# A decoder trunk in split fp32: two more pairs of blocks as seven products, another order of the recurrent steps, and pairs and softplus at other blocks

## Chip, cores and metric

One Trainium2 core runs the kernel in one launch. The metric is device time in microseconds. The kernel before took 1047.36 us as the median of three runs (1046.35 to 1047.64).

## The reference

Two layers work on x of 256 tokens by 1024 features, in float32. Every layer has a feed-forward (SwiGLU), a mixer and a second feed-forward, each followed by a residual sum and a LayerNorm:

```python
x = layer_norm(ALPHA * x + 0.5 * swiglu(x, w_in, w_out), g, b)   # d_ff 2816
x = layer_norm(ALPHA * x + mixer(x), g, b)
x = layer_norm(ALPHA * x + 0.5 * swiglu(x, w_in, w_out), g, b)

def swiglu(x, w_in, w_out):
    gate, up = jnp.split(x @ w_in, 2, axis=-1)
    return (jax.nn.silu(gate) * up) @ w_out
```

The mixer of the first layer is a gated linear recurrence over 1280 channels in five groups of 256: `log_a = -8 * sigmoid(gates0) * softplus(-lam)`, `a = exp(log_a)`, `b = sqrt(-expm1(2 * log_a)) * sigmoid(gates1) * u`, `h = scan(a, b)`, and `(gelu(y) * h) @ w_out`, where u is a short causal convolution. The mixer of the second layer is attention over three dilated windows, on keys and values projected once from the output of the first layer.

## The kernel before

**Products.** Nothing fits in SBUF for long: all weights stream from HBM in halves of 128x1024 float32. Each half is split in two parts of type float32r: the scalar engine (ACT) casts it to the high part (L130), the vector engine (DVE) subtracts that from the original to get the low part (L131). A product is three matmuls, high by high, high by low and low by high (`mm3`, L93). Six buffers hold raw halves and nine the split ones (`RAWBUFS`, `WBUFS`), so ACT and DVE may run up to nine halves ahead of TensorE.

**A feed-forward** (`ffn`, L402) walks over eleven blocks of 256 of its 2816 columns. A normal block j takes four halves of `w_in`, 48 matmuls of 512 columns, then a silu on ACT, the gate on DVE, four transposes, and a split of the result; with it go two halves of `w_out` for block j-2, 24 matmuls into the sums `yy`. The last three pieces of `w_out` come at the end, with the LayerNorm behind them (`Project.finish`).

**Pairs** (`combined` L330, `two_blocks` L438) do two neighbouring blocks together with seven products in place of eight, in Strassen's manner with fewer sums (Winograd's form): a product is 12 matmuls. The halves of the weights that the products need are sums and differences of raw halves, made by DVE in place (L342, eight per pair) and then split as others are (L107, L108: fourteen halves per pair, where two normal blocks have eight). The matching sums of x, `s1` to `s4`, are made once per feed-forward (`sum_x`, L407: eight sums on DVE, four splits). `PAIRS` says which blocks begin a pair: in the first feed-forward 4 and 8, in the second and fourth 3 and 7, in the third none.

**The recurrent part** (L616) runs a list of steps, `RG` (L602), and keeps ACT, DVE and GpSimd in the program's order (`pinned`, L159). `uN` and `yN` are projections (48 matmuls of 256 columns), `cN` the convolution, `gN` the gate products (16 matmuls), `hN` the sigmoids, `bN` the exp and tanh, `aN` a sum on DVE, `qN` the square root, `mN` a product, `sN` the scan, `eN` a copy of y, `zN` its gelu, `FN` the product of both, `kN` its split, `oN` the output projection, which reads what `kN` wrote. `pv` prepares one more half of weights ahead; `pV` does so too, but with the cast on DVE and not on ACT. `T` and its digits say how many halves are prepared at the points of `finish`.

**What sets the order elsewhere.** Outside the pinned parts a list scheduler places the instructions of each engine, by the order of the program and by what is ready in its own reckoning. Each engine then runs its list strictly in that order, and so does the DMA queue of the sync engine. TensorE's list keeps the program's order throughout.

Of the kernel before, what the change touches and what calls it, by code (L numbers as in the profile page):

```python
# [10 lines left out]
F32R = mybir.dt.float32r  # L11
AF = mybir.ActivationFunctionType
ALU = mybir.AluOpType

P = 128
# [13 lines left out]
NO_SYNC = mybir.DependencyInfo(mybir.DependencyClass.NoSync, mybir.DependencyReason.DATA)  # L29
# [6 lines left out]
TAIL = 3  # L36
WBUFS = 9
RAWBUFS = 6
PAIRS = {0: (4, 8), 1: (3, 7), 3: (3, 7)}
KVBUFS = 12  # L40
WARM = 17
PRE = 2
LATE = 5
HBUFS = 6
DILATIONS = ((128, 1), (512, 4), (2048, 16))
SLOPES = [float(2.0 ** (-8.0 * (i + 1.0) / HEADS)) for i in range(HEADS)]
# [3 lines left out]
def trunk_kernel(  # L50
# [21 lines left out]
    nc = tc.nc  # L72
# [3 lines left out]
    act = ctx.enter_context(tc.tile_pool(name="act", bufs=1))  # L76
# [38 lines left out]
    def at(pair, *idx):  # L115
        return pair[0][(slice(None),) + idx], pair[1][(slice(None),) + idx]

    barrier = {}

    def half_piece(src, low=nc.vector, cuts=1, high=nc.scalar):  # L120
        if low is None:
            w = wts.tile([P, HALF], F32, name="w_full", tag="w_hi", bufs=WBUFS)
            nc.sync.dma_start(w, src)
            return w
        raw = wts.tile([P, HALF], F32, name="raw", bufs=RAWBUFS)
        w = duo("w", WBUFS, wts, (HALF,))
        for n in range(cuts):
            c = slice(n * HALF // cuts, (n + 1) * HALF // cuts)
            nc.sync.dma_start(raw[:, c], src[:, c])
            (nc.scalar.copy if high is nc.scalar else high.tensor_copy)(w[0][:, c], raw[:, c])  # L130
            i = low.tensor_tensor(out=w[1][:, c], in0=raw[:, c], in1=f32(w[0][:, c]), op=ALU.subtract)  # L131
        if low in barrier:
            tc.add_manual_dep(i.ins, barrier[low].ins.name, NO_SYNC, reason="after the LayerNorm")
        return w
# [17 lines left out]
    def take(n=2):  # L152

        pump(n - len(ready))
        w, ready[:n] = ready[:n], []
        return w
# [69 lines left out]
    def load_ln(i, tag="o", bufs=4):  # L226
        gb = [[act.tile([P, 512], F32, name="gb", tag=f"{tag}_{('hi', 'lo')[j]}", bufs=bufs) for j in range(2)]
              for _ in range(2)]
        for r in range(2):
            for h in range(2):  # L230
                tc.keep_in_program_order(
                    nc.sync.dma_start(gb[r][h], ln[i, r, h * 512:(h + 1) * 512].partition_broadcast(P)))
        return gb
# [145 lines left out]
    def order_ffn(idx):  # L379
# [4 lines left out]
        for j in range(NJ):  # L384
            if j - 1 in PAIRS.get(idx, ()):
                continue
            if j in PAIRS.get(idx, ()):
                sums = combined(idx, j)
# [10 lines left out]
        for i in range(NJ - TAIL, NJ):  # L399
            order(w_out[idx, i])  # L400

    def ffn(ln_i, turn_x, ahead, pairs=()):  # L402
        hs, gated = {}, {}
        later = []
        sums = {}

        def sum_x():  # L407

            sums["tmp"] = v = [act.tile([P, 4, P], F32, name="v", tag="kv", bufs=KVBUFS) for _ in range(4)]

            def whole(dst_, q, t):
                hi, lo = at(xT, slice(4 * q, 4 * q + 4), tok(t))
                nc.vector.tensor_tensor(dst_, f32(hi), f32(lo), ALU.add)

            def keep(name, src):
                pair = [act.tile([P, 4, P], F32R, name="s", tag="kv", bufs=KVBUFS) for _ in range(2)]
                split(pair[0], pair[1], src)
                sums[name] = pair

            whole(v[0], 0, 0)  # L420
            whole(v[1], 0, 1)
            nc.vector.tensor_tensor(v[2], v[0], v[1], ALU.subtract)
            keep("s3", v[2])
            whole(v[3], 1, 1)
            nc.vector.tensor_tensor(v[1], v[1], v[3], ALU.add)
            keep("s1", v[1])
            nc.vector.tensor_tensor(v[0], v[1], v[0], ALU.subtract)
            keep("s2", v[0])
            whole(v[3], 1, 0)
            nc.vector.tensor_tensor(v[3], v[3], v[0], ALU.subtract)  # L430
            keep("s4", v[3])
# [6 lines left out]
        def two_blocks(j):  # L438

            xs = [act_.rearrange("p k s -> p (k s)") for act_ in sums["tmp"]]  # L440
            flat = lambda n: xs[n]
            part = lambda q, t: (lambda k: at(xT, 4 * q + k, tok(t)))
            named = lambda n: (lambda k: at(sums[n], k))
            a, b, c = (bank() for _ in range(3))
            product(a, part(0, 0), True, False)
            nc.scalar.copy(flat(0), a)
            product(c, named("s1"), True, False)
            nc.scalar.copy(flat(1), c)
            flush()
            product(b, named("s2"), True, False)  # L450
            nc.vector.tensor_tensor(flat(2), b, flat(0), ALU.add)
            product(c, named("s4"), False)
            nc.vector.tensor_tensor(flat(3), c, flat(2), ALU.add)
            gate(flat(3), 0, j + 1)
            w = take()
            for t in range(NT):
                prj.part(t, j - 2, w)
            product(b, named("s3"), False, False)
            nc.vector.tensor_tensor(flat(2), b, flat(0), ALU.add)
            nc.vector.tensor_tensor(flat(1), flat(1), flat(2), ALU.add)  # L460
            gate(flat(1), 1, j + 1)
            product(a, part(1, 0), False)
            gate(a, 0, j)
            product(b, part(1, 1), False)
            nc.vector.tensor_tensor(flat(0), b, flat(0), ALU.add)
            flush()
            gate(flat(0), 1, j)
            w = take()
            for t in range(NT):
                prj.part(t, j - 1, w)  # L470

# [3 lines left out]

        def gate(ps, t, j):
            sg = work.tile([P, 256], F32, name="sg")
            nc.scalar.activation(sg, ps[:, :256], AF.Silu)  # L478
            if t == 0:
                gated[j] = work.tile([P, NT, 256], F32, name="gated", tag="sc")  # L480
            nc.vector.scalar_tensor_tensor(gated[j][:, t, :], ps[:, 256:], 0.5, sg, ALU.mult, ALU.mult)  # L481

            def rest():
                hh = gated.pop(j)
                pt = bank()
                for m in range(2):
                    for t_ in range(NT):
                        turn(pt[:, (m * NT + t_) * P:(m * NT + t_ + 1) * P], hh[:, t_, m * P:(m + 1) * P])
                split(*hs[j], halves(pt))
            if t:  # L490
                later.append(rest)

        prj = Project(lambda t, k: at(hs[k // 2], k % 2, tok(t)), KF)
        for j in range(2):
            hs[j] = duo("h", HBUFS)
        if turn_x:
            gb = load_ln(ln_i)
            w = [take() for _ in range(3)]
            opened = []
            for t in range(NT):  # L500
                ps = bank()
# [5 lines left out]
                ps = bank()  # L507
# [9 lines left out]
        else:  # L517
            with pinned():
                ps = [[bank() for _ in range(NT)] for _ in range(2)]
                for q in range(4):  # L520
# [4 lines left out]
                    for j in range(2):  # L525
                        w = take(1)
# [8 lines left out]
                    if j == 0:  # L535
                        pump(4 - PRE)
        for j in range(2, NJ):
            if j == LATE and not turn_x:
                late_loads()
                gb = load_ln(ln_i)  # L540
                softplus_prep()
            if j - 1 in pairs:
                continue
            hs[j] = duo("h", HBUFS)
            if j in pairs:
                hs[j + 1] = duo("h", HBUFS)
                two_blocks(j)
                continue
            w = [take() for _ in range(2)]
            for t in range(NT):  # L550
                ps = bank()
                natural(ps, t, w)
                flush(1 - t if j == 2 else 0)
                gate(ps, t, j)
            if j == 2 and pairs:
                sum_x()
            if 0 <= j - 2 < NJ - TAIL:
                w = take()
                for t in range(NT):
                    prj.part(t, j - 2, w)  # L560
        for i in range(NJ - 2, NJ - TAIL):
            w = take()
# [21 lines left out]
    def natural_pair(turn_x, then):  # L584
# [3 lines left out]
        for t, ps in enumerate(natural_both(turn_x)):  # L588
# [3 lines left out]
            def rest(t=t, tmp=tmp):  # L592
# [6 lines left out]

    ENGINES = {"v": (nc.vector, nc.scalar), "g": (nc.gpsimd, nc.scalar),  # L600
               "V": (nc.vector, nc.vector), "G": (nc.gpsimd, nc.vector)}
    RG = """pv u3 pv pv pv r0 pv pv r1 c1 pv u2 pv u4 pv c0 g0 pv c2 pv pv c4 pv g1 pv pv h0 h1 pv y0 pv c3 e0 pv  # L602
        g2 h2 b2 y1 pv b0 g3 pv h3 pv pv g4 h4 y2 pv a2 b4 b1 b3 a01 y3 q01 a34 e2 q34 y4 z0 m01 e1 z1 s0 s1
        m4 F1 F0 z2 pv e4 k0 k1 z4 e3 q2 s4 m3 o0 m2 z3 s2 F4 F2 o1 s3 k2 o2 pv F3 pv k4 k3 T21101""".split()

    def order_recurrent():
        both = (nc.vector, nc.vector)
# [349 lines left out]
    order_ffn(3)  # L957

    turn_x = ffn(0, None, 4, PAIRS.get(0, ()))
    with pinned():  # L960
        turn_x = recurrent(1, turn_x)
    turn_x = ffn(2, turn_x, 4, PAIRS.get(1, ()))
    kv = keys_values(turn_x)
    pump(6)
    turn_x = ffn(3, lambda h: None, 4)
    with pinned():
        turn_x = attention(kv, 4, turn_x)
    ffn(5, turn_x, 0, PAIRS.get(3, ()))

# [75 lines left out]
```

## Time and profile before

| what | value |
|---|---|
| median of the runs (three) | 1047.36 us |
| the profiled execution, its own time | 1048.89 us |
| its span, first to last instruction | 1047.1 us |
| TensorE busy | 1019.5 us, 97% |
| DVE busy | 774.5 us, 74% |
| ACT busy | 568.7 us, 54% |
| mean granted clock of TensorE | 0.995 |
| HBM read | 190.75 MB, 183 GB/s over the span |

The stages can be told from the matmuls: first feed-forward to about 194 us, recurrent part to 308, second feed-forward to 495, keys and values to 545, third feed-forward to 725, attention to 858, fourth feed-forward to the end. TensorE is nearly always busy, so the places that count are the few where it waits, and the number of its matmuls. A share of 74% for DVE is a mean over stages between 50% and 97%.

### The profile page before, as it was taken

Reading aid. Unit: us, or ns where it says so; the run is one execution under the profiler, and the core shown is the slowest. Engines: PE = TensorE matmul, PEld = TensorE weight load, DVE = VectorE, ACT = ScalarE, POOL = GpSimd, SP = SyncE. Lnnn points to the kernel's source line nnn. Section 1 sums busy time; section 2 is a strip of 40 time slices with the busy share of each in tenths; the row PEclk is TensorE's granted clock in tenths of the full one; section 3 lists DMA queues with packets and bytes.
Section 4 is the critical chain, followed back from the end, with each engine's and each line's share of the span. In section 5 each row is a group of like instructions: output and inputs, shape, how many; then the busy total and the mean of one; then the engine's idle time right before and its main releaser. Section 6 shows DMA issues by size and latency. Waiting matters only on the chain.

```text
span 1047.1 us, 13806 instructions
## 1 busy us (share of the span) xinstructions
PE 1019.5 (97%) x5233; PEld 853.4 (82%) x5233; DVE 774.5 (74%) x997; ACT 568.7 (54%) x790; POOL 12.0 (1%) x18
## 2 busy tenths in 40 slices
PE   8999999999899999999999999999999999999997
PEld 6787887899777888888898888888998778888885
DVE  6979877686789888777736454557677889888864
ACT  5647555359955564654435344442776755564740
POOL 0000000000000000000000000000000000000000
PEclk9999999999899999999999999999999999999999
DMA  8639458175263483672756555642533544483641
GB/s 300 243 103 339 158 195 305 62 281 173 84 228 141 138 272 140 230 286 101 263 200 203 198 186 177 200 164 99 182 122 121 181 141 151 141 281 132 240 161 41
DMA packets 55650, 192.70 MB, mean 184 GB/s; under 512 B 6432, under 2 KB 6688, under 8 KB 55584
## 3 DMA queue, kind: packets, MB, share of 16 engines
q1 hardware_dynamic: 55584, 191.83, 53.4%
q8 instruction: 41, 0.67, 0.3%
q14 instruction: 25, 0.20, 0.1%
HBM read 190.75 MB, written 1.05 MB: 183 GB/s over the span
## 4 chain that ended last, share of the span: by engine, by line
PE 83%; DVE 7%; ACT 3%; DMA 3%; issue 2%; POOL 0%; SPq 0%; DVEq 0%; ACTq 0%; POOLq 0%
PE mm L91 51%; PE yy L91 29%; PE mm L101 3%; DVE w_lo L131 2%; DMA raw<-in_w_in_dram 2%; DVE w_lo L108 1%; DMA raw<-in_w_out_dram 1%; ACT w_hi L130 1%; DVE xn L257 1%; DVE xT L108 1%; DVE xn L244 1%; DVE st L245 1%; ACT th L104 1%; ACT w_hi L107 0%; ACT L104 0%
## 5 line engine op out<-in xcount | busy, mean ns | idle before, releaser
L131 DVE TENSOR_TENSOR w_lo<-raw,w_hi 128x1024 fp32r<-128x1024 f32 (+1 forms) x295 | 352.1, 1217 | 118.0 <-ACT w_hi L130 111.2
L91 PE MATMUL mm<-w_hi,xT 128*128 128x512 f32 x1296 | 417.6, 393 | 2.6 <-DVE gated L481 1.2
L130 ACT CAST w_hi<-raw 128x1024 fp32r<-128x1024 f32 (+1 forms) x294 | 301.5, 1048 | 178.1 <-PE yy L91 70.6
L91 PEld LDWEIGHTS mm<-w_hi,xT 128*128 128x128 f32 x1296 | 242.8, 188 | 57.3 <-DVE xT L108 2.9
L91 PE MATMUL mm<-w_lo,xT 128*128 128x512 f32 x648 | 253.0, 390 | 2.2 <-DVE w_lo L131 2.2
L91 PEld LDWEIGHTS mm<-w_lo,xT 128*128 128x128 f32 x648 | 121.8, 188 | 28.0 <-DVE w_lo L131 4.0
L91 PE MATMUL yy<-w_hi,h_hi 128*128 128x512 f32 x352 | 138.9, 395 | 0.0
L91 PE MATMUL yy<-w_lo,h_hi 128*128 128x512 f32 x352 | 137.3, 390 | 0.0
L91 PE MATMUL yy<-w_hi,h_lo 128*128 128x512 f32 x352 | 137.3, 390 | 0.0
L107 ACT CAST w_hi<-raw 128x1024 fp32r<-128x1024 f32 x84 | 86.0, 1052 | 65.4 <-DVE raw L342 31.1
L108 DVE TENSOR_TENSOR w_lo<-raw,w_hi 128x1024 fp32r<-128x1024 f32 x84 | 100.6, 1219 | 14.4 <-ACT w_hi L107 14.0
L91 PE MATMUL mm<-xT,w_hi 128*128 128x256 f32 x480 | 88.6, 286 | 0.0
L91 PEld LDWEIGHTS yy<-w_lo,h_hi 128*128 128x128 f32 x352 | 66.2, 188 | 14.1 <-DVE w_lo L131 0.8
L91 PEld LDWEIGHTS yy<-w_hi,h_lo 128*128 128x128 f32 x352 | 66.1, 188 | 13.9
L91 PEld LDWEIGHTS yy<-w_hi,h_hi 128*128 128x128 f32 x352 | 66.1, 188 | 13.1
L91 PEld LDWEIGHTS mm<-xT,w_hi 128*128 128x128 f32 x480 | 74.7, 191 | 2.4 <-issue 2.0
L478 ACT ACTIVATE sg<-mm 128x256 f32<-128x256 f32 x70 | 26.6, 381 | 88.1 <-PE mm L91 87.8
L91 PE MATMUL mm<-xT,w_lo 128*128 128x256 f32 x240 | 67.9, 283 | 0.0
L481 DVE SCALAR_TENSOR_TENSOR gated<-mm,sg 128x256 f32<-128x256 f32 x70 | 29.1, 419 | 47.0 <-ACT sg L478 47.0
L91 PE MATMUL mm<-w_hi,s 128*128 128x512 f32 x192 | 62.7, 393 | 0.0
L342 DVE TENSOR_TENSOR raw<-raw 128x1024 f32<-128x1024 f32 x48 | 57.7, 1218 | 1.8 <-DMA raw<-in_w_in_dram 1.6
L91 PEld LDWEIGHTS mm<-xT,w_lo 128*128 128x128 f32 x240 | 45.9, 191 | 0.0
(132 smaller groups left out, 995.0 us busy)
## 6 DMA issues: line engine op xcount, KB each, us to landing
raw<-in_w_in_dram SPq DMA_DIRECT2D x175, 512.0 KB, 4.9
raw<-in_w_out_dram SPq DMA_DIRECT2D x88, 512.0 KB, 5.0
raw<-in_q_w_dram SPq DMA_DIRECT2D x20, 512.0 KB, 4.5
raw<-in_rg_in_dram SPq DMA_DIRECT2D x16, 512.0 KB, 4.8
gb<-in_ln_dram SPq DMA_DIRECT2D x24, 256.0 KB, 5.7
raw<-in_rg_out_dram SPq DMA_DIRECT2D x10, 512.0 KB, 3.9
raw<-in_v_w_dram SPq DMA_DIRECT2D x8, 512.0 KB, 5.1
raw<-in_k_w_dram SPq DMA_DIRECT2D x8, 512.0 KB, 5.6
```

Of the source, the lines that this page charges most:

```text
L91: tc.keep_in_program_order(nc.tensor.matmul(ps, lhsT=lhsT, rhs=rhs, start=start, stop=stop, **kw))
L101: tc.keep_in_program_order(nc.tensor.transpose(ps, src, ident))
L104: tc.keep_in_program_order(nc.scalar.activation(dst_, src, f, **kw))
L107: nc.scalar.copy(hi, src)
L108: nc.vector.tensor_tensor(lo, src, f32(hi), ALU.subtract)
L130: (nc.scalar.copy if high is nc.scalar else high.tensor_copy)(w[0][:, c], raw[:, c])
L131: i = low.tensor_tensor(out=w[1][:, c], in0=raw[:, c], in1=f32(w[0][:, c]), op=ALU.subtract)
L244: nc.vector.scalar_tensor_tensor(z, z, ALPHA, y, ALU.mult, ALU.add)
L245: nc.vector.bn_stats(self.st[:, h, :], z)
L342: nc.vector.tensor_tensor(raw[out, h], raw[x, h], raw[y, h], ALU.subtract)
L478: nc.scalar.activation(sg, ps[:, :256], AF.Silu)
L481: nc.vector.scalar_tensor_tensor(gated[j][:, t, :], ps[:, 256:], 0.5, sg, ALU.mult, ALU.mult)
```

## The change

Four edits. (1) `PAIRS` gets an entry for the third feed-forward, (3, 7), so four of its blocks are done as two pairs; the sums `s1` to `s4` have their homes in the buffers named o and h there, since keys and values hold eight of the twelve kv buffers. (2) In the first feed-forward the pairs begin at 5 and 8 rather than at 4 and 8, `sum_x` is called before the first pair rather than at block 2, and `softplus_prep` at block 7 rather than 5. (3) `ahead_of`: the first weight half that ACT casts for the block after a pair must come behind the silu of the pair's second block, half t = 1. (4) `RG` is another order of the same steps, with 11 of its 26 `p` steps as `pV`, and T22001 for T21101.

```diff
-PAIRS = {0: (4, 8), 1: (3, 7), 3: (3, 7)}
+PAIRS = {0: (5, 8), 1: (3, 7), 2: (3, 7), 3: (3, 7)}
+SOFTPLUS = 7
...
-            (nc.scalar.copy if high is nc.scalar else high.tensor_copy)(w[0][:, c], raw[:, c])
+            i = (nc.scalar.copy if high is nc.scalar else high.tensor_copy)(w[0][:, c], raw[:, c])
+            if high in ahead_of:
+                tc.add_manual_dep(i.ins, ahead_of.pop(high).ins.name, NO_SYNC, reason="after the gate")
...
-                pair = [act.tile([P, 4, P], F32R, name="s", tag="kv", bufs=KVBUFS) for _ in range(2)]
+                pair = [act.tile([P, 4, P], F32R, name="s", tag=tag, bufs=bufs) for tag, bufs in homes[len(sums) - 1]]
...
-            gate(flat(1), 1, j + 1)
+            silu = gate(flat(1), 1, j + 1)
...
             w = take()
+            ahead_of[nc.scalar] = silu
             for t in range(NT):
                 prj.part(t, j - 1, w)
...
-            if j == LATE and not turn_x:
+            if not turn_x and j == LATE:
                 late_loads()
                 gb = load_ln(ln_i)
+            if not turn_x and j == SOFTPLUS:
                 softplus_prep()
...
-            if j == 2 and pairs:
+            if pairs and j == pairs[0] - 1:
                 sum_x()
...
-    RG = """pv u3 pv pv pv r0 pv pv r1 c1 pv u2 pv u4 pv c0 g0 pv c2 pv pv c4 pv g1 pv pv h0 h1 pv y0 pv c3 e0 pv
...
+    RG = """u4 pv pV pv pv pV pv pv r0 pV r1 u3 C0 u2 c1 pV g0 C2 pv g1 y0 c3 pv pv g2 pV pv h0 C4 pv y1 g4 pv e0
...
-    turn_x = ffn(3, lambda h: None, 4)
+    o_pair, h_pair = (tuple((f"{tag}_{part}", bufs) for part in ("hi", "lo")) for tag, bufs in (("o", 4), ("h", HBUFS)))
+    turn_x = ffn(3, lambda h: None, 4, PAIRS.get(2, ()), 2 * (o_pair,) + 2 * (h_pair,))
```

What this does to the engines' lists is shown at three places. Line numbers of the changed kernel are 1 to 7 higher.

First, ACT at the end of the second pair of the first feed-forward; before:

```order
L107 CAST w_hi<-raw 128x1024 x2
L130 CAST w_hi<-raw 128x1024 x5
L478 ACTIVATE sg<-v 128x256
L478 ACTIVATE sg<-mm 128x256
L130 CAST w_hi<-raw 128x1024 x2
L107 CAST h_hi<-mm 128x512
L478 ACTIVATE sg<-v 128x256
L130 CAST w_hi<-raw 128x1024 x4
```

and of the change:

```order
L108 CAST w_hi<-raw 128x1024 x3
L131 CAST w_hi<-raw 128x1024 x2
L482 ACTIVATE sg<-v 128x256
L482 ACTIVATE sg<-mm 128x256
L131 CAST w_hi<-raw 128x1024 x2
L108 CAST h_hi<-mm 128x512
L131 CAST w_hi<-raw 128x1024
L482 ACTIVATE sg<-v 128x256
L131 CAST w_hi<-raw 128x1024 x6
```

The silu (`sg<-v`) had five casts of weights ahead of it that were not the pair's own products, and has two.

Second, ACT in the recurrent part, from the table load of the square roots (`th<-th`) to the first split of a result that `o0` reads (`kv<-y`); before:

```order
L104 ACT_TABLE_LOAD
L104 ACTIVATE th<-th 128x512 x2
L655 COPY y<-yy 128x512
L104 ACTIVATE th<-th 128x512 x2
L104 ACT_TABLE_LOAD
L104 ACTIVATE y<-y 128x512
L655 COPY y<-yy 128x512
L104 ACTIVATE y<-y 128x512 x2
L130 CAST w_hi<-raw 128x1024
L655 COPY y<-mm 128x512
L107 CAST kv<-y 128x512 x2
```

and of the change:

```order
L105 ACT_TABLE_LOAD
L105 ACTIVATE th<-th 128x512 x4
L105 ACT_TABLE_LOAD
L105 ACTIVATE y<-y 128x512
L661 COPY y<-yy 128x512 x2
L105 ACTIVATE y<-y 128x512 x2
L108 CAST kv<-y 128x512
```

A cast of weights and a copy that stood before the split are gone from there. Earlier on the list, a block's exp and tanh (four instructions) and the casts between the last sigmoids and the table load have moved ahead of the last sigmoids or to DVE. DVE's list from its last sums (`iu<-aa,iu`) to the low part of the same split, of the change:

```order
L701 SCALAR_TENSOR_TENSOR iu<-aa,iu 128x512 x2
L709 TENSOR_TENSOR iu<-iu,th 128x512 x2
L714 SCALAR_TENSOR_TENSOR th<-aa,iu 128x256 x2
L709 TENSOR_TENSOR iu<-iu,th 128x512
L719 TENSOR_TENSOR y<-y,th 128x512
L714 SCALAR_TENSOR_TENSOR th<-aa,iu 128x256 x2
L131 CAST w_hi<-raw 128x1024
L134 TENSOR_TENSOR w_lo<-raw,w_hi 128x1024
L719 TENSOR_TENSOR y<-y,th 128x512
L109 TENSOR_TENSOR kv<-y,kv 128x512
```

A cast of weights stands in it now, beside the split of weights that stood there before too.

Third, DVE in the first blocks of the program, around the last sums of x (`v<-v` and `s<-v,s`) and the first gates; before:

```order
L427 TENSOR_TENSOR v<-v 128x512
L413 TENSOR_TENSOR v<-xT_73,xT_74 128x512
L430 TENSOR_TENSOR v<-v 128x512
L108 TENSOR_TENSOR s<-v,s 128x512 x2
L481 SCALAR_TENSOR_TENSOR gated<-mm,sg 128x256 x2
```

and of the change:

```order
L430 TENSOR_TENSOR v<-v 128x512
L416 TENSOR_TENSOR v<-xT_73,xT_74 128x512
L433 TENSOR_TENSOR v<-v 128x512
L109 TENSOR_TENSOR s<-v,s 128x512 x2
L485 SCALAR_TENSOR_TENSOR gated<-mm,sg 128x256 x2
```

Nothing moved here: though the call stands at a later block, the scheduler puts the sums where they stood.

## Rows read from the trace of the kernel before

**Rows 1.** Page, part 1: busy us, share of the span, instructions.
```profile
PE 1019.5 (97%) x5233; PEld 853.4 (82%) x5233; DVE 774.5 (74%) x997; ACT 568.7 (54%) x790; POOL 12.0 (1%) x18
```
**Rows 2.** Timeline of TensorE: start, us, instruction, [idle before, what ended it].
```profile
32.48 0.50 PE L91 MATMUL mm<-w_hi,xT 128*128 128x512 f32 x1 [1.23 <-DVE gated L481]
...
92.86 0.55 PE L101 MATMUL mm<-ident,gated 128*128 128x128 f32 x3 [0.95 <-DVE gated L481]
...
159.69 0.55 PE L101 MATMUL mm<-ident,gated 128*128 128x128 f32 x3 [2.12 <-DVE gated L481]
...
276.09 0.80 PE L91 MATMUL yy<-w_hi,kv 128*128 128x512 f32 x1 [4.66 <-ACT kv L107]
...
304.54 0.66 PE L101 MATMUL mm<-ident,xn 128*128 128x128 f32 x4 [1.07 <-DVE xn L257]
```
**Rows 3.** Chain of waits in order of time: start, us, what.
```profile
254.17 4.21 PE yy L91 x35
...
276.09 24.68 PE yy L91 x96
...
344.74 5.47 PE yy L91 x24
...
376.00 5.79 PE yy L91 x24
...
409.96 5.44 PE yy L91 x24
...
440.79 5.49 PE yy L91 x24
...
572.79 5.49 PE yy L91 x24
...
707.27 2.72 PE yy L91 x12
```
**Rows 4.** Stretches: us; busy of PE, PEld, DVE, ACT, POOL; clock; DMA; GB/s.
```profile
272.00:289.00 17.00, 12.91 (x45) 10.33 (x46) 15.64 (x23) 14.95 (x22) 0.00 (x0) 0.80 0.22 71
...
425.00:442.00 17.00, 17.00 (x78) 14.09 (x77) 15.81 (x19) 11.20 (x14) 0.00 (x0) 1.00 0.72 245
...
578.00:595.00 17.00, 17.00 (x79) 14.07 (x78) 8.71 (x9) 7.67 (x10) 0.00 (x0) 1.00 0.54 176
```
**Rows 5.** Groups by line: xcount | busy us, mean ns of one | idle before.
```profile
L131 DVE TENSOR_TENSOR w_lo<-raw,w_hi 128x1024 fp32r<-128x1024 f32 (+1 forms) x295 | 352.1, 1217 | 118.0 <-ACT w_hi L130 111.2
```
**Rows 6.** Groups by line and shape.
```profile
L104 ACT ACTIVATE aa<-th,sp 128x256 f32<-128x256 f32 x10 | 5.0, 498 | 0.0
...
L130 DVE CAST w_hi<-raw 128x1024 fp32r<-128x1024 f32 x1 | 0.7, 687 | 0.0
```
**Rows 7.** Timeline of ACT, first feed-forward.
```profile
55.58 0.39 ACT L478 ACTIVATE sg<-mm 128x256 f32<-128x256 f32 x1 [4.18 <-PE mm L91]
...
89.13 1.28 ACT L478 ACT_TABLE_LOAD   x1
90.42 0.42 ACT L478 ACTIVATE sg<-v 128x256 f32<-128x256 f32 x1
...
157.81 1.04 ACT L130 CAST w_hi<-raw 128x1024 fp32r<-128x1024 f32 x1 [1.92 <-DMA raw<-in_w_in_dram]
158.76 0.41 ACT L478 ACTIVATE sg<-v 128x256 f32<-128x256 f32 x1
```
**Rows 8.** Timeline of DVE, the same place.
```profile
155.15 0.68 DVE L460 TENSOR_TENSOR v<-v 128x512 f32<-128x512 f32 x1
```
**Rows 9.** Timeline of ACT, recurrent part.
```profile
255.77 0.87 ACT L104 ACTIVATE th<-mm,par 128x256 f32<-128x256 f32 x2
...
258.39 1.05 ACT L130 CAST w_hi<-raw 128x1024 fp32r<-128x1024 f32 x1 [1.03 <-PE yy L91]
...
274.01 1.03 ACT L130 CAST w_hi<-raw 128x1024 fp32r<-128x1024 f32 x1
...
275.42 1.14 ACT L107 CAST kv<-y 128x512 fp32r<-128x512 f32 x2
```

More of the change, by code (lines that the diff above doesn't have):

```diff
@@ L116, in at @@
         return pair[0][(slice(None),) + idx], pair[1][(slice(None),) + idx]
-    barrier = {}
+    barrier, ahead_of = {}, {}
     def half_piece(src, low=nc.vector, cuts=1, high=nc.scalar):
@@ L400, in order_ffn, with ffn @@
             order(w_out[idx, i])
-    def ffn(ln_i, turn_x, ahead, pairs=()):
+    def ffn(ln_i, turn_x, ahead, pairs=(), homes=4 * (2 * (("kv", KVBUFS),),)):
         hs, gated = {}, {}
@@ L477, in gate @@
             sg = work.tile([P, 256], F32, name="sg")
-            nc.scalar.activation(sg, ps[:, :256], AF.Silu)
+            silu = nc.scalar.activation(sg, ps[:, :256], AF.Silu)
             if t == 0:
@@ L491, in gate @@
                 later.append(rest)
+            return silu
         prj = Project(lambda t, k: at(hs[k // 2], k % 2, tok(t)), KF)
@@ L601, in trunk_kernel @@
                "V": (nc.vector, nc.vector), "G": (nc.gpsimd, nc.vector)}
-    RG = """pv u3 pv pv pv r0 pv pv r1 c1 pv u2 pv u4 pv c0 g0 pv c2 pv pv c4 pv g1 pv pv h0 h1 pv y0 pv c3 e0 pv
-        g2 h2 b2 y1 pv b0 g3 pv h3 pv pv g4 h4 y2 pv a2 b4 b1 b3 a01 y3 q01 a34 e2 q34 y4 z0 m01 e1 z1 s0 s1
-        m4 F1 F0 z2 pv e4 k0 k1 z4 e3 q2 s4 m3 o0 m2 z3 s2 F4 F2 o1 s3 k2 o2 pv F3 pv k4 k3 T21101""".split()
+    RG = """u4 pv pV pv pv pV pv pv r0 pV r1 u3 C0 u2 c1 pV g0 C2 pv g1 y0 c3 pv pv g2 pV pv h0 C4 pv y1 g4 pv e0
+        pv pV h1 h2 b2 g3 y2 pV b1 pv b0 pV a01 y4 pV h4 h3 a2 b3 b4 q01 pV a34 m01 s0 q34 y3 z0 E2 e1 z1 m4
+        F0 z2 s1 pV F1 K0 E4 z4 s4 e3 K1 q2 F4 z3 o0 m2 m3 s2 o1 K4 F2 pv s3 k2 F3 pv o2 k3 T22001""".split()
     def order_recurrent():
```

## Prediction

> **What bounds the kernel now.** I read the page's first part, then TensorE's own timeline for the places where it waits, then the chain for the length of a block, and last the lists of ACT and DVE at those places. TensorE is busy for 1019.5 of the span's 1047.1 us [rows 1], so an edit counts in two ways only: it takes matmuls away, or it takes one of TensorE's few waits away. In full stretches matmuls of 512 columns follow each other at 5.44 / 24 = 0.227 us by the row at 409.96 [rows 3]. The waits that touch the edits are these [rows 2]: 1.23 us at 32.48 (first gates of the program), 0.95 at 92.86 and 2.12 at 159.69 (the transposes at the end of the two pairs of the first feed-forward), 4.66 at 276.09 (the recurrent part's first output projection waits for ACT's split `kv`) and 1.07 at 304.54 (its LayerNorm). Behind the wait of 4.66 something else is lost: the next 96 matmuls take 24.68 us [rows 3], where 96 x 0.227 = 21.8 would do, and the granted clock of that stretch is 0.80 where the others show 1.00 [rows 4]; the level below 2.4 GHz is 1.2. That wait costs 4.66 + 2.9, of which I count 2.8.
>
> **Third feed-forward.** Eight normal blocks there go from 572.79 to 707.27 [rows 3]: 134.48 / 8 = 16.81 us each, 33.62 for two. A pair has 84 matmuls of `w_in` for 96, so 12 x 0.227 = 2.72 less. What it gets is shown by the second feed-forward: from one `w_out` to the one behind the pair, 344.74 to 376.00 is 31.26 us and 409.96 to 440.79 is 30.83 [rows 3], 2.36 and 2.79 below two normal blocks. The third has pairs at the same blocks, so I take both: **-5.15**. The work that pays for it lies on DVE. Two normal blocks hold 33.62 x 8.71 / 17 = 17.2 us of DVE, by the stretch at 578 [rows 4]; a pair adds six splits of halves (7.3) and eight differences of the same size (9.7) at 1.217 us [rows 5], and five sums of 0.68, as the one of their size [rows 8], 3.4: 37.6 us in a stretch of 31. The 6.6 us that are missing come out of the lead of nine split halves: half a product's weights feed six matmuls, 1.36 us, so nine cover 12.2. A normal block gives back 16.81 - 8.6 = 8.2. In the second feed-forward DVE is busy 15.81 of 17 us in a pair and TensorE 17.00 [rows 4], so the cover is there; the third begins with a DVE that has idled more. Bounds: -5.45 with nothing lost, above zero if the lead is gone (a rival below). The sums of x (eight of 0.68 on DVE) fall in its first blocks, where half of DVE is free: nothing.
>
> **First feed-forward.** The sums of x do not move, as the list of DVE shows, so the wait of 1.23 at 32.48 stays: 0. The pair's last wait is one of order. TensorE needs the gate of half t = 1; that needs a silu, and ACT's silu at 158.76 stood behind a cast that itself waited 1.92 us for its DMA until 157.81 [rows 7], though its input, the DVE sum of 155.15, was done by 155.83 [rows 8]. With only two casts ahead of it, both of the pair's own `w_out`, the silu runs near 156, the gate follows behind one split that DVE has in hand (1.22), and is done about 157.4; TensorE came at 159.69 - 2.12 = 157.57. I leave 0.2 of the 2.12. At the first pair softplus with its two table loads (1.28 for the one at 89.13) stood before the silu of 90.42 [rows 7] and the gate; it now lies a block before the pair, in a stretch where ACT had 4.18 us idle ahead of a silu [rows 7]. Its loads and two small steps fill 3.0 of them. ACT may also have to wait there for the parameters' DMA, which is issued late in that block; what is queued behind is a silu and the split of the block before, which `w_out` reads some 5 us later. I take 0, with up to 1.5 as the bad end. Moving the first pair one block back leaves one normal block between the pairs where there were two; it gives back 8.2 us of DVE against the 6.6 that the pair took, so the second pair begins with a smaller lead, but with one. Sum: -0.95 - 2.12 + 0.2 = **-2.9**, bounds 0 and -3.1. In the second and fourth feed-forward the same rule moves one or two casts behind a silu; TensorE does not wait at those places, so nothing.
>
> A rule of the Trainium skill speaks against that 0: "ScalarE: Activation LUTs", section "What ACT_TABLE_LOAD costs", counts a drain of about 1.38 us beside every load, 2.66 for a switch. By it softplus would fill 5.7 us, 1.5 more than the idle stretch, and the sum would be -1.4 at worst in place of -2.9. In the trace the silu at 90.42 starts 1.29 us after the load at 89.13 [rows 7], so the measured price stands.
>
> **Recurrent part.** TensorE has the same steps in both orders, and in both three projections, 17.3 us, follow the last gate product, which ends at 254.17 [rows 3]. So it comes to `o0` at the same 276.09 - 4.66 = 271.43. The question is when ACT and DVE have the first `kv`. Before: the last sigmoids (four instructions) began at 255.77 and ended at 258.39 - 1.03 = 257.36, 1.59 us; then came a wait of 1.03 and a cast of 1.05, and the table load at 259.46; then three blocks of exp and tanh, roots, gelus; the split began at 275.42 [rows 9]. In the changed list the casts before the last sigmoids and behind them are gone, so these run from 254.2 to 255.8 and the table load follows: 3.65 earlier. Two blocks of exp and tanh are left for three: four instructions of 0.498 [rows 6] less, 1.95. The cast and the copy from 274.01 to 275.42 are behind the split now: 1.41. Sum 7.0: the high part begins at 268.4 and ends at 269.0, 2.4 us before TensorE. The low part is tighter. From 255.8 there are a table load (1.28), eight instructions of exp and tanh (4.0), a second load (1.28) and the first root (0.57, half of the two casts of its size at 275.42, rows 9): 262.9. DVE then has ten steps of at most 0.68, a cast of 0.687 [rows 6] and a split of 1.217 [rows 5] up to the low part: 8.7, so 271.6; overlaps between neighbours make it less. TensorE needs it with its third matmul, at 271.43 + 0.45 = 271.9. So the 4.66 goes, and with it the low clock: -4.66 - 2.8. `o1` to `o4` read parts that are made at least 3 us ahead by the same count. T22001 puts two splits where one stood between the two halves of the first LayerNorm, so the second half may start 1.0 later and the wait of 1.07 at 304.54 grows; the split that stood behind that LayerNorm is gone in turn, which returns most. I take +0.3. Sum **-7.2**; bounds 0 (the wait only changes its cause) and -7.5.
>
> **Sum.** The profiled execution took 1048.89 us, 1.79 beside its span and 1.53 more than the median. -5.15 - 2.9 - 7.2 = -15.25: 1033.6 for it, **1032.1** for the median.
>
> **Rivals.** (A) The first `kv` is late all the same: the low part has 0.3 us to spare by full durations, with a dozen hand-overs between ACT and DVE before it. Each microsecond late is one of waiting; at 2.5 the time is 1034.6, and if the whole of 7.2 is lost, 1039.3. For it: the list is nearly without gaps from 254 to 269. Against it: overlaps, and 2.4 us of reserve on ACT. (B) The waits of the first feed-forward stay under another name, since the second pair has one block of recovery in place of two, or the parameters come late: +2.9, 1035.0. For it speaks that DVE's stretch of 37.6 now comes twice within 79 us; against it that both waits come from a place in a list, which is seen to move. (C) The slower side: DVE sets the pace of pairs. It decides where the lead at a pair's start is under the 6.6 us that the pair takes out, five halves. Then a pair of the third feed-forward takes DVE's 37.6 us in place of 33.6, +4.0 each, and the second pair of the first +6.6: 1047.36 + 8.0 + 6.6 - 7.2 - 0.95 = 1053.8. Against it stand both pairs of the second feed-forward, which had no wait.
>
> **Chances.** Forecast 0.62, A 0.18, B 0.12, C 0.08. All but C are faster; of C I give 0.03 to a draw, where only one pair is late. About 0.2% (2 us) is what a measurement of this kernel can tell from no change. Faster 0.92, same 0.03, slower 0.05. The range: from 1030.0 (bounds of the three sums, -17, with a little for shorter waits in the other pairs) to 1037.5, which takes in A and B but for their worst; about 0.15 is left out.
>
> **What would show it.** In the trace of the changed kernel: yy to yy across a pair in the third feed-forward 30.8 to 31.3 us with no TensorE wait on `w_lo`; the two waits on `gated` at the pairs' ends under 0.3 us; no wait over 0.5 before `o0`, and a granted clock of 1.00 through the stretch behind it; the wait of 1.2 near 32 us unchanged. I am wrong if a wait on `kv` of over 2 us remains, if TensorE waits for `w_lo` inside a pair, or if DVE in the third feed-forward is full for a whole pair and the block behind it.

## The result and the profile after

The changed kernel took 1031.12 us (median of four runs, 1030.45 to 1032.00), the kernel before, measured beside it, 1047.30: ratio 0.9847, 95% interval 0.983 to 0.9864, or 16.2 us less. 15.25 less was forecast, and 1032.1 us. The profiled execution took 1031.31 us with a span of 1029.5, which is 17.6 under the span of before.

Page of the changed kernel, part 1, against [rows 1]:

```profile
PE 1011.0 (98%) x5209; PEld 847.9 (82%) x5209; DVE 822.4 (80%) x1055; ACT 573.9 (56%) x802; POOL 11.9 (1%) x18
```

TensorE has 24 instructions less (two pairs, 12 matmuls each) and 8.5 us less work; DVE has 47.9 us more. The rest of the gain is time in which TensorE had waited or run slowly. Its timeline at the places of [rows 2] (start, us, instruction, [idle before, what ended it]):

```profile
31.12 0.50 PE L92 MATMUL mm<-w_hi,xT 128*128 128x512 f32 x1 [1.22 <-DVE gated L485]
...
293.45 0.66 PE L102 MATMUL mm<-ident,xn 128*128 128x128 f32 x4 [1.94 <-DVE xn L260]
...
360.69 0.47 PE L92 MATMUL mm<-w_hi,xT 128*128 128x512 f32 x1 [0.38 <-DVE v L462]
```

The waits of 0.95, 2.12 and 4.66 us have no row any more; the 1.2 us at the first gates is there as before, the LayerNorm's wait has grown from 1.07 to 1.94, and one of 0.38 in a pair of the second feed-forward is new. The chain of waits passes the old place of the 4.66 without a break, and the stretches of [rows 4] read 1.00:

```profile
261.25 24.84 PE yy L92 x132
```

```profile
272.00:289.00 17.00, 17.00 (x77) 14.08 (x76) 15.65 (x20) 10.45 (x13) 0.00 (x0) 1.00 0.58 182
...
578.00:595.00 17.00, 17.00 (x78) 14.08 (x78) 16.03 (x20) 10.82 (x15) 0.00 (x0) 1.00 0.76 262
```

The second row is inside a pair of the third feed-forward: DVE went there from 8.71 to 16.03 of 17 us, and TensorE is still full. The pairs themselves, on the same chain (yy before and behind each):

```profile
561.13 5.47 PE yy L92 x24
...
592.01 5.47 PE yy L92 x24
...
625.65 5.44 PE yy L92 x24
...
656.51 5.47 PE yy L92 x24
```

That is 30.88 and 30.86 us, for 33.62 of two normal blocks. Stage by stage, from TensorE's timeline (the marks are the first gates, the first transposes of each LayerNorm, `mm<-ident,xn`, the first transposes of the recurrent part, `mm<-ident,nat`, and `o0`):

| from, to | before | after | difference | forecast |
|---|---|---|---|---|
| start, first gates | 32.48 | 31.12 | -1.36 | 0 |
| first gates, end of first feed-forward | 158.51 | 155.42 | -3.09 | -2.9 |
| that, first transposes of the recurrent part | 21.85 | 21.87 | 0 | 0 |
| those, `o0` | 63.25 | 58.44 | -4.81 | -4.66 |
| `o0`, end of recurrent part | 28.45 | 26.60 | -1.85 | -2.5 |
| second feed-forward | 183.83 | 183.25 | -0.58 | 0 |
| keys and values, third feed-forward | 232.82 | 227.38 | -5.44 | -5.15 |
| attention, fourth feed-forward | 325.91 | 325.42 | -0.49 | 0 |

The 1.36 us at the start are put down to chance: in the profiles of the twelve experiments, all with the same work up to there, the first gates came between 30.43 and 31.61 us. The profile of before is the late one, and its execution lay 1.5 over its median. Without it 16.2 us are left, as between the medians.

### The profile page after: what moved, and what is told of

The parts are those of the page before. It is cut to its first block, busy times and chain, and to the rows that moved or that the text cites. A ratio compares the mean times of both kernels' runs of the same rounds, so it can differ in the third digit from the quotient of the medians.

```text
span 1029.5 us, 13804 instructions
## 1 busy us (share of the span) xinstructions
PE 1011.0 (98%) x5209; PEld 847.9 (82%) x5209; DVE 822.4 (80%) x1055; ACT 573.9 (56%) x802; POOL 11.9 (1%) x18
## 4 chain that ended last, share of the span: by engine, by line
PE 87%; DVE 7%; ACT 2%; DMA 2%; issue 1%; SPq 0%; POOL 0%; DVEq 0%; ACTq 0%; POOLq 0%
PE mm L92 54%; PE yy L92 30%; PE mm L102 3%; DVE w_lo L134 2%; DMA raw<-in_w_in_dram 1%; DVE w_lo L109 1%; DVE raw L345 1%; DVE xn L260 1%; DVE xn L247 0%; ACT w_hi L131 0%; DVE xT L109 0%; DVE st L248 0%; DMA raw<-in_w_out_dram 0%; ACT w_hi L108 0%; ACT sc L871 0%
## 5 line engine op out<-in xcount | busy, mean ns | idle before, releaser
L134 DVE TENSOR_TENSOR w_lo<-raw,w_hi 128x1024 fp32r<-128x1024 f32 (+1 forms) x279 | 332.6, 1217 | 84.8 <-ACT w_hi L131 82.1
L92 PE MATMUL mm<-w_hi,xT 128*128 128x512 f32 x1216 | 392.2, 394 | 2.4 <-DVE gated L485 1.2
L131 ACT CAST w_hi<-raw 128x1024 fp32r<-128x1024 f32 (+1 forms) x270 | 275.3, 1047 | 134.6 <-PE yy L92 47.6
L92 PE MATMUL mm<-w_lo,xT 128*128 128x512 f32 x608 | 237.9, 391 | 1.3 <-DVE w_lo L134 1.3
L108 ACT CAST w_hi<-raw 128x1024 fp32r<-128x1024 f32 x112 | 114.8, 1052 | 94.0 <-DVE raw L345 45.9
L109 DVE TENSOR_TENSOR w_lo<-raw,w_hi 128x1024 fp32r<-128x1024 f32 x112 | 134.5, 1220 | 25.3 <-ACT w_hi L108 24.7
L92 PE MATMUL mm<-w_hi,s 128*128 128x512 f32 x256 | 83.7, 393 | 0.0
L345 DVE TENSOR_TENSOR raw<-raw 128x1024 f32<-128x1024 f32 x64 | 76.9, 1219 | 2.7 <-DMA raw<-in_w_in_dram 2.5
L92 PEld LDWEIGHTS yy<-w_lo,h_hi 128*128 128x128 f32 x352 | 66.2, 188 | 13.6 <-DVE w_lo L134 0.6
L92 PEld LDWEIGHTS mm<-w_hi,s 128*128 128x128 f32 x256 | 48.1, 188 | 9.9
L92 PE MATMUL mm<-w_lo,s 128*128 128x512 f32 x128 | 49.9, 390 | 0.0
```

Of the source, the lines that this page charges most:

```text
L92: tc.keep_in_program_order(nc.tensor.matmul(ps, lhsT=lhsT, rhs=rhs, start=start, stop=stop, **kw))
L108: nc.scalar.copy(hi, src)
L109: nc.vector.tensor_tensor(lo, src, f32(hi), ALU.subtract)
L131: i = (nc.scalar.copy if high is nc.scalar else high.tensor_copy)(w[0][:, c], raw[:, c])
L345: nc.vector.tensor_tensor(raw[out, h], raw[x, h], raw[y, h], ALU.subtract)
```

## The experiments

Four kernels make one part of the change alone, three vary the recurrent part of the changed kernel, and the others ask how many pairs DVE and its buffers can carry.

**Third feed-forward alone.**

```diff
-PAIRS = {0: (4, 8), 1: (3, 7), 3: (3, 7)}
+PAIRS = {0: (4, 8), 1: (3, 7), 2: (3, 7), 3: (3, 7)}
...
-    turn_x = ffn(3, lambda h: None, 4)
+    turn_x = ffn(3, lambda h: None, 4, PAIRS.get(2, ()), 2 * (o_pair,) + 2 * (h_pair,))
```

> The kernel before with one edit alone, the two pairs of the third feed-forward (3 and 7). Theory (a pair saves 12 x 0.227 = 2.72 us of matmuls and DVE's extra 6.6 us come out of the lead): 5.2 to 5.5 us less than before, about 1042.1 us; yy to yy across each pair 30.8 to 31.3 us, no TensorE wait on w_lo. Rival (DVE sets the pace of a pair): 4 us more per pair, 1051 to 1055 us, with waits on w_lo inside the pairs.

1041.28 us, ratio 0.9944 (0.9927 to 0.996). Its stage took 228.20 us, 4.6 less than before and 0.8 more than in the full change. No wait on `w_lo`, but one on a gate at the first pair's end, which the theory did not have:

```profile
602.93 0.55 PE L102 MATMUL mm<-ident,gated 128*128 128x128 f32 x3 [0.61 <-DVE gated L484]
```

On ACT two casts stood there waiting for DMAs ahead of the silu, as in the first feed-forward. In the full change, which has the rule on the silu, this wait has no row; so the rule looks worth about 0.6 us in the third one too.

**Order of the recurrent part alone.**

```diff
-    RG = """pv u3 pv pv pv r0 pv pv r1 c1 pv u2 pv u4 pv c0 g0 pv c2 ...
+    RG = """u4 pv pV pv pv pV pv pv r0 pV r1 u3 C0 u2 c1 pV g0 C2 pv ...
```

> The kernel before with the new order of the recurrent steps alone. Theory (the first kv is ready before TensorE comes, and the low clock behind the wait goes with the wait): 7.2 to 7.9 us less, about 1039.8 us, granted clock 1.00 from the last projection to o4. Rival (kv is late for another reason): a wait of 2 us or more stays before o0, 1042 to 1047 us. Second rival (the low clock of the 17 us behind has another cause than the wait): the wait of 4.66 goes, the clock stays near 0.8, 1042.7 us.

1041.45 us, ratio 0.9939 (0.9919 to 0.996). `o0` came 58.43 us after the first transposes, 58.44 in the full change: the wait is gone with this edit alone, and the stretch behind it ran at 1.00, so the low clock went with the wait. Two other waits were followed by a lower clock here, the one at the second pair's end (2.21 us, left as before) and the LayerNorm's 1.94:

```profile
153.00:170.00 17.00, 14.79 (x62) 11.92 (x61) 14.13 (x16) 9.35 (x12) 0.00 (x0) 0.90 0.76 262
272.00:289.00 17.00, 17.00 (x77) 14.05 (x76) 15.64 (x21) 14.30 (x17) 0.00 (x0) 1.00 0.34 123
289.00:306.00 17.00, 15.06 (x64) 12.11 (x63) 13.96 (x21) 5.10 (x7) 0.99 (x1) 0.90 0.63 236
```

A tenth of 17 us is 1.7 us for each, by estimate, and it hides part of this edit's gain in this execution (1043.76 us; the six runs lie between 1038.54 and 1044.12). The interval, 4.2 to 8.5 us less, takes in the 7.2 to 7.9 that was expected.

**The rule on the silu alone**, and **the moved pairs, sums and softplus without it**:

```diff
+            if high in ahead_of:
+                tc.add_manual_dep(i.ins, ahead_of.pop(high).ins.name, NO_SYNC, reason="after the gate")
...
+            ahead_of[nc.scalar] = silu
```

> The kernel before with the rule alone that ACT casts the next block's weights only behind the silu of a pair's second block. Theory (the 2.12 us at the end of the second pair of the first feed-forward are a matter of place in ACT's list): that wait falls under 0.3, the 0.95 us at the first pair stay since softplus still stands before its silu, about 1.9 us less, 1045.4 us. Rival (the wait goes over to DVE's list or to the weights of the next block, which are now cast later): 1047.4 us, with a new wait on w_hi or w_lo behind the pair.

```diff
-PAIRS = {0: (4, 8), 1: (3, 7), 3: (3, 7)}
+PAIRS = {0: (5, 8), 1: (3, 7), 3: (3, 7)}
+SOFTPLUS = 7
...
-            if j == 2 and pairs:
+            if pairs and j == pairs[0] - 1:
```

> The kernel before with the first feed-forward's pairs at 5 and 8, the call of the sums of x before the first pair and softplus at block 7, without the rule on the silu. Theory (only softplus caused the 0.95 us; the 2.12 us need the rule): 0.95 us less, about 1046.4 us, a wait of about 2 us at the end of the second pair still there. Rival (the later first pair takes away DVE's recovery between the pairs): up to 2.9 us more, 1049 us, with waits on w_lo in the second pair.

The rule alone: 1045.59 us, ratio 0.9974 (0.9964 to 0.9984), the 2.12 us gone, 1.03 left at the first pair, as expected. The moved pairs alone: 1047.61 us, ratio 0.9999 (0.9987 to 1.0011), so no gain that the runs can tell; the interval, 1.4 us less to 1.2 more, doesn't rule out the 0.95 that was expected. The profile shows that only part of it came:

```profile
107.66 0.55 PE L102 MATMUL mm<-ident,gated 128*128 128x128 f32 x3 [0.60 <-DVE gated L484]
...
157.60 0.55 PE L102 MATMUL mm<-ident,gated 128*128 128x128 f32 x3 [1.46 <-DVE gated L484]
```

The wait at the first pair is 0.60 us for 0.95, the one at the second 1.46 for 2.12, and the stage took 158.10 us for 158.51. In the kernel before, the next cast of weights stood behind the first pair's silus (it began at 93.06). With softplus away and the pair one block later, two casts stand ahead of the silu, each waiting about 1 us for its DMA, and the silu begins only at 106.74. So one delay went and another took its place; only the two edits together take the wait away. The rival (waits on `w_lo` in the second pair) did not show either.

**The casts on ACT again.** Same order of steps, every `pV` made `pv`.

> The changed kernel with all eleven casts that the recurrent part gives to DVE (pV) on ACT again (pv), same order of steps. Theory (the first kv is in time because casts left ACT): two casts of 1.04 us lie between the last sigmoids and the first split, the others push the sigmoids back; ACT had 3.1 us in hand, so the wait before o0 is 0 to 5 us, likeliest 2, and 1.7 to 3 us of low clock behind it where the wait is over 2: 1033 to 1038 us. Rival (the order of the steps did it, the casts are free on either engine): no wait, 1031.1 us.

1042.46 us, ratio 0.9955 (0.9942 to 0.9969). TensorE's timeline:

```profile
271.16 0.80 PE L92 MATMUL yy<-w_hi,kv 128*128 128x512 f32 x1 [4.59 <-ACT kv L108]
274.01 1.22 PE L92 MATMUL yy<-w_hi,kv 128*128 128x512 f32 x2 [1.63 <-DVE kv L109]
```

The whole wait is back, and a second one, of the low part, with it; the clock is 0.79 from 272 to 289. ACT's own list shows the cast of weights and the split that `o0` waits for:

```profile
269.47 1.03 ACT L131 CAST w_hi<-raw 128x1024 fp32r<-128x1024 f32 x1
270.49 0.62 ACT L108 CAST kv<-y 128x512 fp32r<-128x512 f32 x1
```

and the same split in the changed kernel:

```profile
263.31 0.61 ACT L108 CAST kv<-y 128x512 fp32r<-128x512 f32 x1
```

TensorE would have come at 266.57 and 266.85. So with all its casts on ACT the new order is worth nothing at `o0`, which comes 63.18 us after the first transposes (63.25 before); with eleven of them on DVE the whole wait goes. Whether the old order with these casts on DVE would do as well was not run. ACT is the engine without slack here: from 244 to 261 it is busy for 16.66 of the 17 us in the changed kernel and DVE for 14.26; with the casts on ACT they are at 16.68 and 8.00. The time lies above the theory's 1033 to 1038, which had a wait of likeliest 2 us. Counted from the first transposes, ACT's table load behind the last sigmoids comes 5.65 us later than in the changed kernel, and two casts of 1.03 stand behind it; less the 2.9 us that ACT had in hand this is 4.8, near the wait of 4.59.

**Splits in the LayerNorm.** T21101, and T31001 (three halves ahead, one between, none behind), for T22001.

> The changed kernel with T21101 in place of T22001 (one prepared half between the two halves of the recurrent part's first LayerNorm in place of two). Theory: the wait of 1.94 us before the LayerNorm's transposes goes back to 1.1, and one of about 1.1 comes at the second LayerNorm's transposes, which are now waited for again: 0.2 us either way, 1031 to 1031.4 us. Rival (the split behind the LayerNorm now stands in no one's way, since the order before it is another): 0.9 us less, 1030.2 us.

> The changed kernel with T31001 in place of T22001: three prepared halves ahead of the recurrent part's last sums, one between the halves of its LayerNorm, none behind the first half's. Theory (one split of 1.2 us between the halves costs 0.9 us of the LayerNorm's wait, one behind it costs 1.1 us of the second LayerNorm's): wait 1.07 before the first transposes and none before the second, 0.9 us less, 1030.2 us. Rival (the third half delays the last sums' own splits or the weights that the last projection needs): a wait on kv or w_lo of 0.5 us or more, no gain.

T21101 took 1032.12 us, ratio 0.9855 (0.9841 to 0.987), with waits of 1.07 and 1.01 us; from `o0` to the end of the second feed-forward 209.94 us against 209.85: the same, as its theory had it. T31001 took 1031.09 us, ratio 0.9832 (0.9817 to 0.9847): one wait,

```profile
292.52 0.66 PE L102 MATMUL mm<-ident,xn 128*128 128x128 f32 x4 [1.07 <-DVE xn L260]
```

and 209.04 us over the same stretch. The 0.8 us are read from the profile; the medians, 1031.09 and 1031.12, don't show them.

**Three pairs in the third feed-forward.** Next to each other, and with a normal block between:

```diff
-PAIRS = {0: (5, 8), 1: (3, 7), 2: (3, 7), 3: (3, 7)}
+PAIRS = {0: (5, 8), 1: (3, 7), 2: (3, 5, 7), 3: (3, 7)}   # close
+PAIRS = {0: (5, 8), 1: (3, 7), 2: (2, 5, 8), 3: (3, 7)}   # apart
```

> The changed kernel with three pairs in the third feed-forward that follow each other, at 3, 5 and 7. Theory (the lead of 12.2 us pays for one pair and most of the second, 2 x 6.6 = 13.2, and for nothing of the third): TensorE waits about 1 us in the second pair and 6.6 in the third, on w_lo; minus 2.7 of matmuls that is 4.9 us more than the changed kernel, about 1036 us; DVE busy all through the second and third pair. Rival (DVE's own time for a pair is under TensorE's 30.9 us): no waits, 1028.5 us.

> The changed kernel with three pairs in the third feed-forward, at 2, 5 and 8, one normal block between each two (the sums of x before block 2). Theory (a pair takes 6.6 us out of the lead of 12.2, one normal block gives 8.2 back): a third saving of 2.4 to 2.8 us, about 1028.5 us, no wait on w_lo over 0.5 us. Rival (the lead isn't what carries a pair, or block 2 comes too early for the sums of x): waits on s or w_lo of 3 us or more, 1031 us or more.

Close: 1050.75 us, ratio 1.0033 (1.002 to 1.0046), the stage 246.50 us. TensorE waited 11.3 us in the two later pairs where 7.6 were counted, and the clock fell behind the waits. But DVE was not full while TensorE waited:

```profile
595.00:612.00 17.00, 14.47 (x64) 11.09 (x62) 14.51 (x14) 7.00 (x9) 0.00 (x0) 1.00 0.32 110
612.00:629.00 17.00, 15.19 (x52) 11.56 (x53) 13.77 (x16) 9.78 (x13) 0.00 (x0) 0.80 0.67 230
629.00:646.00 17.00, 15.03 (x67) 11.45 (x65) 14.56 (x15) 8.24 (x11) 0.00 (x0) 1.00 0.28 93
646.00:663.00 17.00, 12.04 (x34) 8.66 (x35) 13.63 (x15) 8.39 (x9) 0.00 (x0) 0.76 0.38 130
```

13.6 to 14.6 of 17, so neither the theory (DVE busy all through) nor the rival (no waits) was right. The issues of the DMA queue show what was short (start, us over which they lie, count):

```profile
597.40 0.33 SPq L342 DMA_DIRECT2D raw<-in_w_in_dram  x1
608.25 1.46 SPq L130 DMA_DIRECT2D raw<-in_w_out_dram  x2
```

For 10.5 us no load was issued. The queue's own waits from 597 to 680 us say what for (us in total, times, longest): a raw buffer that a split on DVE had to free first.

```profile
SPq L130 <- DVE w_lo L109: 26.4, 9, 10.4
```

The halves whose differences were still to be made held the six buffers; then each half went through DMA, cast and split one after the other, with TensorE waiting at the end. Apart: 1032.28 us, ratio 0.9852 (0.9833 to 0.987); the third pair has the same gap (no issue from 640.9 to 652.04) and waits of 0.98, 0.75 and 0.58 us behind it, so the third saving is lost: 228.27 us for the stage.

**A seventh raw buffer**, with five for h to make room, under both of these:

```diff
-RAWBUFS = 6
+RAWBUFS = 7
-HBUFS = 6
+HBUFS = 5
```

> The kernel with pairs at 3, 5 and 7 in the third feed-forward, with seven buffers for raw halves in place of six (and five in place of six for h, which makes the room). Theory (what paces pair behind pair is the ring of raw halves: a difference must free a raw buffer before the next DMA is issued, 3.3 us from issue to landing, then a cast and a split): the third feed-forward, 246.5 us from LayerNorm to LayerNorm with six, takes 6 to 12 us less, and the stretches without an issue of a DMA get shorter. Rival (DVE's throughput paces it, 37.6 us for a pair): 246 to 247 us again.

> The kernel with pairs at 2, 5 and 8 in the third feed-forward, with seven raw buffers and five for h. Theory (the 0.98, 0.75 and 0.58 us of waits in the third pair come from the same ring): these waits go, the third feed-forward takes 224.6 to 226 us from LayerNorm to LayerNorm (228.3 with six, 227.4 with two pairs), the whole about 1028.5 us. Rival (fewer buffers for h stall the pairs, or the third pair has no lead on any count): 228 us or more there, 1032 us or more.

Close: 1040.03 us, ratio 0.9915 (0.99 to 0.993), the stage 235.81 us, 10.7 less than with six, but still 8.4 over the two pairs of the changed kernel, with 7.3 us of waits in the later pairs. Apart: **1027.26 us, ratio 0.9799 (0.9784 to 0.9814)**, the stage 224.65 us, and TensorE without a wait through the third pair:

```profile
633.00:650.00 17.00, 17.00 (x79) 14.06 (x78) 15.04 (x16) 8.68 (x10) 0.00 (x0) 1.00 0.35 113
650.00:667.00 17.00, 17.00 (x77) 14.05 (x76) 15.90 (x19) 9.94 (x14) 0.00 (x0) 1.00 0.79 253
```

224.65 is 2.73 under the two pairs of the changed kernel, which is the third pair's 12 matmuls. Another 1.2 us come in the second feed-forward, 182.04 us for 183.25. This version beats both kernels. Its work on DVE is that of the kernel with six buffers, so DVE's throughput was not what made the third pair wait, and the ring of raw halves is what the rows point at. The gaps in the DMA queue stay nearly as long, though the theory had them shorter: 10.5 us with close pairs as before, 9.2 for 11.1 with pairs apart. But a first half of `w_out`, which with six buffers is issued behind the gap, is now issued ahead of it, at 596.08 and 635.02. Two other things changed with the ring and were not run by themselves: five buffers for h, and the scheduler's order, which differs a little (in the third pair apart three differences stand in a row on DVE, two with six buffers).

**Three pairs in the second and fourth feed-forward too**, with T31001:

> The kernel with seven raw buffers (five for h) and pairs at 2, 5 and 8 in the second and fourth feed-forward too, not in the third alone, with T31001. Theory (three pairs with one normal block between each two go without a wait only where DVE has made a lead before the first; in the first 34 us of the second feed-forward DVE is busy 33.0, in the third's only 19.6): TensorE waits at the pair at 2 for up to the 6.6 us that the pair takes out, so the second feed-forward (182.0 us from LayerNorm to LayerNorm) and the fourth (191.9 to the end) take 1 to 4 us more each, the third stays at 224.7, T31001 gives 0.9 back: 1028 to 1034 us. Rival (the seventh raw buffer was all that was missing): both take 2.7 us less, about 1021 us.

1031.56 us, ratio 0.9846 (0.9826 to 0.9867), slower than the version above. Second feed-forward 184.06 us for 182.04, attention and fourth 327.27 for 325.68, third 224.66 as before. The stretch ahead of the second one's first pair, and the pair:

```profile
309.00:326.00 17.00, 17.00 (x80) 14.06 (x79) 16.95 (x23) 8.63 (x14) 0.00 (x0) 1.00 0.26 90
326.00:343.00 17.00, 14.45 (x62) 10.84 (x61) 16.58 (x17) 9.92 (x12) 0.00 (x0) 1.00 0.52 179
```

Here DVE is the one that is full, TensorE waits 2.55 us, and the saving is gone. In the fourth one the waits are 2.4 us for 0.6, and the wait before the transposes of attention's LayerNorm is 2.46 us for 1.45. T31001 did not give all of its 0.9 back: a wait of 0.89 stands at the second LayerNorm's transposes. The time lies inside the theory's 1028 to 1034; the waits are smaller than its 6.6.

## Why the prediction was right

**Third feed-forward, -5.15, measured -5.44.** The like pairs of the second one gave the size; what came is twice the 12 matmuls of a pair, the bound with nothing lost. The account behind it (DVE's 6.6 us a pair from a lead of 12.2) was not what sets the limit. Two pairs with two normal blocks between them never met it; three in a row met one, and there TensorE waited while DVE was at 13.6 to 14.6 of 17 us, behind a stretch in which the DMA queue issued nothing. Rival C, with DVE's pace as its price, did not happen in this change; with three pairs in a row a slower kernel exists (1050.75 us), and in the second feed-forward DVE did become full.

**First feed-forward, -2.9, measured -3.09.** Both waits went and the first one stayed, as worked out. The place in ACT's list was the right cause at the second pair. At the first one softplus was the cause, but hardly by the table loads that the prediction names: the silu that they held up began at 90.42, 0.1 us after its input was ready. What came late was the gate, behind the small steps of softplus on DVE, in the kernel before:

```profile
89.62 0.69 DVE L460 TENSOR_TENSOR v<-v 128x512 f32<-128x512 f32 x1
...
91.29 1.19 DVE L219 SCALAR_TENSOR_TENSOR spt<-spt 128x10 f32<-128x10 f32 x6
92.39 0.42 DVE L481 SCALAR_TENSOR_TENSOR gated<-v,sg 128x256 f32<-128x256 f32 x1
```

The silu ended at 90.84, the gate began 1.55 us later, and TensorE would have come at 91.91. Nor was softplus enough: without the rule on the silu 0.60 us of the wait stay, so the -0.95 came out by an edit that the prediction did not count on at this pair. The cost of nothing for softplus held: ACT waited 3.51 us for the parameters and TensorE did not notice.

```profile
53.60 0.21 ACT L214 ACTIVATE spt<-par 128x10 f32<-128x10 f32 x1 [3.51 <-DMA par<-in_rg_par_dram]
53.83 1.28 ACT L215 ACT_TABLE_LOAD   x1
55.13 0.21 ACT L215 ACTIVATE spt<-spt 128x10 f32<-128x10 f32 x1
```

The step behind a load starts 1.30 us after it, so no drain beside the load is seen. The Trainium skill, "ScalarE: Activation LUTs", section "What ACT_TABLE_LOAD costs", would have 2.66; the measured 1.30 decides.

**Recurrent part, -7.2, measured -7.24** from the first transposes to the end of the second feed-forward, with its terms a little off each. `o0` moved by 4.81 (4.66 forecast). The high part was ready 2.9 us before TensorE (2.4 forecast), the low part 1.0 us before its matmul (0.3 forecast): its split on DVE is

```profile
265.60 0.69 DVE L109 TENSOR_TENSOR kv<-y,kv 128x512 fp32r<-128x512 f32 x1
```

and ends at 266.29, while the third matmul of `o0` is due at 266.85 + 0.45. From `o0` to the end of the recurrent part 1.85 us went, not 2.5: without the low clock 2.7 came back (2.8 forecast), and the LayerNorm's wait took 0.87 more, not 0.3. In return a wait at the second LayerNorm is gone, which the prediction had no row for; in the kernel before it was

```profile
314.95 0.63 PE L101 MATMUL mm<-ident,xn 128*128 128x128 f32 x4 [1.10 <-DVE xn L257]
```

That -7.24 lies so near -7.2 is luck in part, since these misses cancel. Counted from the first transposes, the terms 3.65, 1.95 and 1.41 measured 4.40, 1.88 and 1.40. They aren't gains of their own: with the casts on ACT the order gives nothing.

**Sum.** -15.25 forecast, -16.2 measured. The missing 1.0 is 0.2 in the first feed-forward, 0.3 in the third and 0.5 in the last stages. In the third the pairs alone gave 4.6, under the 5.15; most of the rest goes with the rule on the silu, which was counted at nothing outside the first, so the nearness there is luck in part. The 0.5 stays open: the waits of TensorE in the last stages add up to 4.2 us in both profiles, and the fourth feed-forward took between 191.57 and 192.78 us in all thirteen profiles with two pairs there. Rivals A and B did not happen. A's reserve was real but hung on the eleven casts: without them the time is 1042.46 us, beyond A's worst of 1039.3.

## What to carry over

Where an engine runs its list in order, look for everything that stands ahead of the instruction that is late, on each engine that it passes through, and look again after an edit: where one delay is taken away, the scheduler may put another in its place. A share of 80% for the engine that prepares data doesn't say what its next piece of work costs; count the buffers that a step holds while it waits, and look in the issues of the DMA queue at what stands ahead of a gap and what behind it. A new order of steps may be worth nothing until work has also left the engine that has no slack.

## What the runs showed of the hardware

The granted clock behind waits of about 2 us is not the same each time. Behind waits of 4.6 us before `o0` it was 0.79 to 0.81 in the stretch from 272 to 289 us in all five profiles that had them. Behind eleven waits of 1.9 to 2.5 us that stood alone it fell in six and stayed at 1.00 in five; behind the wait of 1.07 before the same LayerNorm, in seven profiles, it never fell. The same wait of 1.94, in the changed kernel and in the one with three pairs apart and six buffers:

```profile
289.00:306.00 17.00, 14.75 (x70) 11.50 (x69) 15.84 (x26) 8.18 (x10) 1.90 (x2) 1.00 0.49 190
```

```profile
289.00:306.00 17.00, 15.06 (x66) 12.15 (x65) 15.19 (x24) 8.17 (x10) 1.90 (x2) 0.90 0.49 191
```

ACT's work there is the same. From these transposes to the end of the second feed-forward the one took 183.25 us and the other 184.47. The Trainium skill, "TensorE: Matmul & The Clock Gate", section "HAM oscillation — how this bites in real kernels", says that a wait for data (there a DMA) can lower the clock and leave the next work at half rate. The second kernel's timeline agrees, with matmuls of 512 columns 0.42 us apart behind the wait (the level of 1.2 GHz) and 0.23 later (that of 2.4):

```profile
295.23 0.63 PE L92 MATMUL yy<-w_lo,kv 128*128 128x512 f32 x1
295.65 0.63 PE L92 MATMUL yy<-w_hi,kv 128*128 128x512 f32 x1
...
298.88 0.39 PE L92 MATMUL mm<-w_hi,xT 128*128 128x512 f32 x1
299.11 0.39 PE L92 MATMUL mm<-w_lo,xT 128*128 128x512 f32 x1
```

The two rows of 17 us add that at 2 us it may or may not happen. It makes single profiles of such a kernel differ by a microsecond or two, which is as much as some of the edits here are worth.
